# A per-token scale ratio, the first silus next to each other, and an earlier forget gate in a streaming-encoder block on one core

## The chip, the core and the metric

The kernel runs on one core of a Trainium2 chip. A core has TensorE (PE, matrix products, with PEld for its weight loads), VectorE (DVE), ScalarE (ACT), GpSimd (POOL) and SyncE (SP), each with its own queue that it takes in order, and 16 DMA engines that all queues share. SP issues the loads of weights, POOL some small or broadcast transfers. The metric is the device time of one execution in microseconds (us), as the median of several runs; the profile shows one execution of its own.

## What is computed

One layer of an encoder block on 256 tokens of 1024 features, in float32:

```python
x = x + 0.5 * rmsnorm(swiglu(rmsnorm(x, g1), ffn1_w_in, ffn1_w_down), g2)   # FFN 1, 2816 wide
q_a, f_a, i_a, g_a, q_b, k_b, v_b, f_b, gates = split(rmsnorm(x, g3) @ w_in)
A = rmsnorm(hgrn2(q_a, f_a, i_a)) * silu(g_a)        # gated linear recurrence, 8 heads
B = fox_attention(q_b, k_b, v_b, f_b + bias)         # causal; logits get the running sums of log f
y = sigmoid(gate_A) * (A @ w_branch_a) + sigmoid(gate_B) * (B @ w_branch_b)
x = x + rmsnorm(y @ w_out)
x = x + rmsnorm(cross_attention(rmsnorm(x), rmsnorm(mem)))
x = x + 0.5 * rmsnorm(swiglu(rmsnorm(x), ffn2_w_in, ffn2_w_down))           # FFN 2
# swiglu(h, w_in, w_down): gate, up = split(h @ w_in); (silu(gate) * up) @ w_down
# fox: c = cumsum(log_sigmoid(f_b + bias)); s[t, s'] = q.k / sqrt(128) + c[t] - c[s']
```

## The kernel before

**Weights.** Each float32 operand is split into a rounded part `hi` and a remainder `lo`, and a product is made of three: hi·hi, hi·lo and lo·hi. A unit of weights is 128x1024: `load_split` (L141) lets SP load it into one of 4 `raw` buffers (L148), ACT cast it to `hi` (L150) and DVE subtract to get `lo` (L152); there are 8 buffers for each of `hi` and `lo`. The subtraction gives `raw` back, which lets SP issue the next load. An entry in `hold` for a unit queues its cast and its subtraction behind two given instructions of ACT and DVE (`behind`); this orders the issue only, and only against instructions of the same engine.

**Order.** A scheduler orders each engine's queue by the program's order and by when it thinks inputs are ready. `tc.high_priority()` moves instructions ahead of others, `tc.issue_after(ins)` queues what follows on `ins`'s engine behind it, and `after(i)` does both against the i-th matmul in the log of PE.

**FFN.** `ffn` (L424) works in chunks of 256 of the 2816 hidden columns, 4 units each, 11 chunks. FFN 1 begins with `act_first`, which makes chunks 0 and 1 in all four `acc` banks while the first weights arrive, and then chunk 2 in the two `mm` banks. A chunk's sums are turned into activations by `act_evac` (L444): ACT's silu (L446) of the gate, scaled by the token's root-mean-square factor, then DVE's product with the other half (L449 or L451) into a tile `at`. `flush` (L432) has PE transpose `at` (L441) and ACT and DVE split the result into `act`, which `down` multiplies with the down weights `w_dn`. `h` counts the two halves of 128 tokens. `TOKS` lists the chunks made by tokens (`act_tok`), `PAIRS` those made two at a time by `act_pair`, a fast product of 2x2 blocks with seven block products in place of eight: FFN 1 has pairs from chunks 4, 6 and 9, FFN 2 from 3, 6 and 9.

A pair combines both halves of the tokens, which have different scales in each token. So `pair_inputs` (L520) first multiplies the second half of `xf` by the ratio of the halves' scales, `rho` (L528), and `act_evac` undoes a ratio `q` later. `row_of` (L354) makes the scales into a row: DVE transposes a 128x64 tile (L357), POOL writes it to memory (L359) and reads it back into all 128 partitions (L361). `rho` is then a reciprocal (L522) and a product (L523) on 128x128; `q` is the same ratio on 128x1 (L525, L526). In `act_pair` the third of four results is `c00` (L636), and its silu and `at` follow; behind a pair that is not followed by another pair comes a chunk by tokens.

**Recurrence and attention.** After FFN 1 the projections follow, with the recurrence's levels (1, 2, 4 to 128) between them: `Rec.grow` multiplies on DVE (L991), `Rec.keep` copies on ACT (L1030, L1034, L1037). The forget logits of the attention are made by `forget` (L1062: ACT's exponential and logarithm, L1070, L1071) and summed by `forget_sums` (L1073) in three DVE instructions (L1074, L1079 twice), whose result POOL writes to memory as `cd` (L1080). POOL later reads `cd` back as `ct` (L1167), `cbc` (L1169) and `cbm` (L1173); `cbc` and each of two `cbm` are 512 KB, broadcast to 128 partitions into buffers of the pool `m4`, which has 21 of 128x1024.

The recurrence's output is summed in `acc` banks, squared on ACT (L290), and multiplied into `G` by DVE (L1159); only then are the banks free for the scores of the attention's second half (L1199), which the rest of the attention reads. The second half of the `v_b` weights is cast meanwhile.

Of the kernel before, what the change touches and what calls it, by code (L numbers as in the profile page):

```python
# [11 lines left out]
F32 = mybir.dt.float32  # L12
# [3 lines left out]
ALU = mybir.AluOpType  # L16
AX = mybir.AxisListType

P = 128
# [4 lines left out]
FC = 256  # L24
GF = 344
NFF = D_FF // FC
# [49 lines left out]
_AT = {}  # L76
# [8 lines left out]
def block_kernel(ctx: ExitStack, tc: tile.TileContext, wts, head_in, gf_in, x_in, mem_in, memT_in, cols, rows, fbias, masks, out):  # L85
    nc = tc.nc
    V, S, G, PE = nc.vector, nc.scalar, nc.gpsimd, nc.tensor

    cp = ctx.enter_context(tc.tile_pool(name="consts", bufs=1))
    wp = ctx.enter_context(tc.tile_pool(name="weights", bufs=4))  # L90
    mp = ctx.enter_context(tc.tile_pool(name="data", bufs=21))
    sp = ctx.enter_context(tc.tile_pool(name="small", bufs=8))
# [16 lines left out]
    def nm(s):  # L109
        count[0] += 1  # L110
        return f"{s}_{count[0]}"
# [21 lines left out]
    evicted = []  # L133
    hold = {}
# [115 lines left out]
    def bc(a, shape, dim):  # L250
        return a.unsqueeze(dim).to_broadcast(shape)
# [89 lines left out]
        return r  # L341


    facs = cp.tile([P, 4, 64], F32, name="facs")
    G.memset(facs, 0.0)
    fac = [facs[:, i] for i in range(4)]

# [3 lines left out]
    def x_halves(h):  # L351
        return [xs[:, h, 0:512], xs[:, h, 512:]]

    def row_of(cols2):  # L354

        runs = sp.tile([P, 64], F32, tag="runs", name=nm("runs"), bufs=1)
        V.transpose(runs, cols2)  # L357
        rd = dp.tile([2, 4, 32], F32, name=nm("rd"))
        G.dma_start(rd.rearrange("h k t -> k h t"), runs[0:P:32].rearrange("k (h t) -> k h t", h=2))  # L359
        row = sp.tile([P, T], F32, tag="row", name=nm("row"), bufs=2)  # L360
        G.dma_start(row, rd.rearrange("h k t -> (h k t)").partition_broadcast(P))  # L361
        return row

    def gain_split(X, kb, src, g, a=0, b=T, first=False):
# [59 lines left out]
    def ffn(w_in, w_dn, X, r2, n_tok, i_row, first_half, second_half=None):  # L424

        acts = {}
        late = []
        ats = {}  # L430

# [12 lines left out]
        def act_evac(ps, c, h, r=None, q=None):  # L444
            sg = sp.tile([P, FC], F32, tag="c1", name=nm("sg"), bufs=7)
            silu = S.activation(sg, ps[:, :FC], AF.Silu, scale=r2[h] if r is None else r).ins  # L446
            a = sp.tile([P, FC], F32, tag="c1", name=nm("at"), bufs=7)
            if q is None:
                V.tensor_tensor(out=a, in0=ps[:, FC:], in1=sg, op=ALU.mult)  # L449
            else:  # L450
                V.scalar_tensor_tensor(out=a, in0=ps[:, FC:], scalar=q, in1=sg, op0=ALU.mult, op1=ALU.mult)  # L451
            ats[c, h] = a
            if h == 1:
                late.append(c)
            return silu
# [61 lines left out]
                V.tensor_tensor(out=t[:, 2 * i : 2 * i + 2], in0=x[:, :, 0], in1=x[:, :, 1], op=ALU.add)  # L517
            return t

        def pair_inputs():  # L520
            rho = sp.tile([P, P], F32, tag="c1", name=nm("rho"), bufs=7)
            V.reciprocal(rho, row[:, :P])  # L522
            V.tensor_tensor(out=rho, in0=row[:, P:], in1=rho, op=ALU.mult)  # L523
            q = s1(name="q")
            V.reciprocal(q, r2[1])  # L525
            V.tensor_tensor(out=q, in0=r2[0], in1=q, op=ALU.mult)  # L526
            for k in range(2):
                V.tensor_tensor(out=xf[k][:, :, P:], in0=xf[k][:, :, P:], in1=bc(rho, [P, 4, P], 1), op=ALU.mult)  # L528
            a, b, d, e = (xf[k][:, :, h * P : h * P + P] for h in range(2) for k in range(2))
            ss = [m4([P, 2, 4, P], n="ss") for _ in range(2)]  # L530
            de, aed, ad, baed = (t[:, i] for t in ss for i in range(2))
            V.tensor_tensor(out=de, in0=d, in1=e, op=ALU.subtract)
            V.tensor_tensor(out=aed, in0=de, in1=a, op=ALU.subtract)
            V.tensor_tensor(out=ad, in0=a, in1=d, op=ALU.subtract)
            V.tensor_tensor(out=baed, in0=b, in1=aed, op=ALU.add)
            out = {}
            for n, x in (("de", de), ("aed", aed), ("baed", baed), ("ad", ad), ("e", e)):
                t = m4([P, 2, 4, P], F32R, "sx")
                split(t[:, 0], t[:, 1], x)
                out[n] = t  # L540
            return out, q
# [16 lines left out]
        def act_pair(c, between):  # L558
            sx, q = pairs_in

            def of(n):
                return lambda kk: (sx[n][:, 0, kk], sx[n][:, 1, kk])

            def of_x(k):
                return lambda kk: (X.hi(4 * k + kk, 0, P), X.lo(4 * k + kk, 0, P))

            def splits(t):
                u = []
                for r in t:
                    p = parts_of()  # L570
                    split(p[0], p[1], r)
                    u.append(p)
                return u

            def raws(k, n):
                t = [wp.tile([P, D], F32, tag="raw", name=nm("raw"), bufs=4) for _ in range(2)]
                for j in range(2):
                    more(t[j], c, k, n, j, None)
                return t

            def add(t, o):
                for x, y in zip(t, o):
                    V.tensor_tensor(out=x, in0=x, in1=y, op=ALU.add)  # L583

            def product(ps, stat, u, start):
                for kk in range(4):
                    ah, al = stat(kk)
                    wh, wl = blk(u, kk)
                    for i, (x, y) in enumerate(((ah, wh), (ah, wl), (al, wh))):
                        MM(ps, x, y, start=start and kk == 0 and i == 0, stop=kk == 3 and i == 2, skip_group_check=not start)  # L590

            def step_between():
                if between:
# [12 lines left out]
            for _ in range(2 if c == 3 else 1):  # L606
                step_between()
            b4 = mm()
            product(b4, of("de"), splits(sums), True)
            S.copy(p5, b4)  # L610
            step_between()
            raw = raws(1, 1)
            add(sums, raw)
            product(b1, of("aed"), splits(sums), False)
            S.copy(v, b1)
            step_between()
            product(b4, of("baed"), splits(raw), False)
            add(both, raw)
            with tc.high_priority():
                t = half_tile("c01")  # L620
                V.tensor_tensor(out=t, in0=b4, in1=v, op=ALU.subtract)
                act_evac(t, c, 0)
            product(b1, of("ad"), splits(both), False)
            S.copy(w, b1)
            with tc.high_priority():
                t = half_tile("c11")
                V.tensor_tensor(out=t, in0=p5, in1=w, op=ALU.subtract)
                act_evac(t, c, 1, r2[0], q)
            step_between()
            b0 = trp()  # L630
            raw = raws(1, 0)
            product(b0, of_x(1), splits(raw), True)
            add(sums, raw)
            with tc.high_priority():
                t = half_tile("c00")
                V.tensor_tensor(out=t, in0=p1, in1=b0, op=ALU.add)  # L636
                act_evac(t, c + 1, 0)
            step_between()
            product(b1, of("e"), splits(sums), False)
            with tc.high_priority():  # L640
                silu = act_evac(b1, c + 1, 1, r2[0], q)
            if c + 1 == NFF - 1:
                table(silu)
            while between:
                step_between()
# [10 lines left out]
        for h in range(2):  # L656
            m = len(log)
            for c in range(n_tok):
                act_tok(c, h)
            if h == 0 and n_tok:  # L660
                second_half(m)
                row = row_of(fac[3])
                if pairs:
                    xf = [pair_joined(k) for k in range(2)]
        accs = None
        done = 0
        if callable(r2):
            outs = act_first((0, 1), acc)
            r2 = r2()
            chunk(w_in, 2)  # L670
            row = row_of(fac[2])
            for c in range(2):
                acts[c] = m4([P, 2, 2, T], F32R, "act")
                for h in range(2):
                    with tc.issue_after(casts[-1]):
                        act_evac(outs[c][h], c, h)
            n_tok = 2
        for c in range(n_tok, NFF):
            if c - 1 in pairs:
# [16 lines left out]
            elif c == 2 and first_half:  # L696
                n = len(log)
# [410 lines left out]
    for si, ms in enumerate(SETS):  # L1108
# [11 lines left out]
                for r in recs:  # L1120
                    r.keep(m, LEVELS.index(m) if m < 64 else None)
        if si == FG:
            with tc.issue_after(recs[1].grown):
                forget_sums()
        if si < 2:
            with tc.high_priority(), tc.issue_after(gf_last[R_GROW[si]]):
# [457 lines left out]
```

## Time and profile before

| | us |
|---|---|
| median of 3 runs | 778.22 |
| lowest and highest run | 776.54, 779.0 |
| the profiled execution, its own time | 779.33 |
| its span, first to last instruction | 777.2 |
| PE busy, weight loads busy | 764.9, 647.1 |
| DVE busy | 646.1 |
| ACT busy | 503.2 |
| POOL busy | 15.7 |
| mean granted TensorE clock | 0.998 |

PE's busy time holds the matmuls' own waits in its pipeline; whether it stands still is seen best from the distance between the starts of matmuls. In rows of instructions the columns are start and duration in us, engine, line, operation, output and inputs, shape and count; in brackets, the engine's idle time just before, and what ended it.

### The profile page before, as it was taken

How to read it: one execution, taken by the hardware profiler on the slowest of the kernel's cores; microseconds unless marked ns; L12 is line 12 of the kernel's file. 1: busy time of each engine (PE TensorE's matmuls, PEld its weight loads, DVE VectorE, ACT ScalarE, POOL GpSimd, SP SyncE). 2: the span in 40 equal slices, each digit the busy share in tenths (PEclk: the TensorE clock that was granted, in tenths of full speed). 3: DMA queues.
4: the chain of work that ended last, by engine and by line, in shares of the span. 5: the costliest groups of instructions: out<-in, count | busy, mean ns of one | idle time of the engine just before them, and what ended most of it. 6: DMA issues, size and time to landing. Idle time of an engine off the chain costs nothing.

```text
span 777.2 us, 11694 instructions
## 1 busy us (share of the span) xinstructions
PE 764.9 (98%) x4326; PEld 647.1 (83%) x4326; DVE 646.1 (83%) x975; ACT 503.2 (65%) x816; POOL 15.7 (2%) x39
## 2 busy tenths in 40 slices
PE   9999999999999999999999999999999999999996
PEld 8878888877888998888788888889888888888885
DVE  6699999988778898969777655886579899999973
ACT  7676666677775669547676444863668567675762
POOL 0000000000000100210000000000000000000000
PEclk9999999999999999999999999999999999999999
DMA  9764657366755535643767555456075725658231
GB/s 343 237 244 159 221 180 298 109 217 205 221 177 146 183 134 177 204 182 133 259 238 255 176 176 192 148 178 222 22 245 177 258 85 176 258 177 318 101 135 55
DMA packets 44505, 148.06 MB, mean 191 GB/s; under 512 B 5144, under 2 KB 8864, under 8 KB 44448
## 3 DMA queue, kind: packets, MB, share of 16 engines
q1 hardware_dynamic: 43168, 144.83, 53.7%
q0 software_dynamic: 848, 2.12, 1.1%
q8 instruction: 34, 0.56, 0.3%
q10 hardware_dynamic: 432, 0.37, 0.2%
q14 instruction: 23, 0.19, 0.1%
HBM read 146.24 MB, written 1.06 MB: 190 GB/s over the span
## 4 chain that ended last, share of the span: by engine, by line
PE 68%; DVE 21%; DMA 4%; issue 3%; ACT 3%; DVEq 0%; ACTq 0%; SPq 0%
PE mm L99 34%; PE acc L99 30%; DVE lo L152 5%; DVE lo L171 5%; DMA raw<-in_wts_dram 3%; DVE sraw L583 3%; PE tr L99 2%; ACT hi L150 1%; DVE qf L991 1%; PE tr L382 1%; DVE k L991 1%; PE tr L441 1%; DMA sraw<-in_wts_dram 1%; DVE act L171 1%; ACT f L1029 0%
## 5 line engine op out<-in xcount | busy, mean ns | idle before, releaser
L152 DVE TENSOR_TENSOR lo<-raw,hi 128x1024 fp32r<-128x1024 f32 (+1 forms) x204 | 241.0, 1200 | 35.7 <-ACT hi L150 30.6
L150 ACT CAST hi<-raw 128x1024 fp32r<-128x1024 f32 (+1 forms) x204 | 206.9, 1035 | 67.9 <-PE mm L99 30.6
L99 PE MATMUL mm<-hi,hlT 128*128 128x512 f32 (+1 forms) x688 | 209.4, 382 | 0.1
L99 PEld LDWEIGHTS mm<-hi,hlT 128*128 128x128 f32 x688 | 127.2, 188 | 22.8 <-issue 0.5
L99 PE MATMUL mm<-lo,hlT 128*128 128x512 f32 (+1 forms) x344 | 130.5, 382 | 0.0
L99 PE MATMUL acc<-hi,act 128*128 128x512 f32 x352 | 113.7, 391 | 0.0
L170 ACT CAST hi<-sraw 128x1024 fp32r<-128x1024 f32 x60 | 62.8, 1053 | 32.1 <-DVE sraw L583 23.2
L99 PE MATMUL mm<-hi,sx 128*128 128x512 f32 x240 | 77.7, 390 | 0.0
L99 PEld LDWEIGHTS acc<-hi,act 128*128 128x128 f32 x352 | 66.1, 188 | 13.4 <-ACT hi L150 0.2
L99 PEld LDWEIGHTS mm<-lo,hlT 128*128 128x128 f32 x344 | 64.6, 188 | 11.2 <-DVE lo L152 0.5
L171 DVE TENSOR_TENSOR lo<-sraw,hi 128x1024 fp32r<-128x1024 f32 x60 | 71.9, 1222 | 2.2 <-ACT hi L170 2.0
L99 PE MATMUL acc<-lo,act 128*128 128x512 f32 x176 | 70.0, 398 | 0.3 <-DVE lo L152 0.3
L99 PE MATMUL acc<-hlT,hi 128*128 128x512 f32 x256 | 64.4, 393 | 0.0
L99 PEld LDWEIGHTS mm<-hi,sx 128*128 128x128 f32 x240 | 45.0, 188 | 9.8 <-ACT sx L170 0.2
L99 PEld LDWEIGHTS acc<-hlT,hi 128*128 128x128 f32 x256 | 46.1, 189 | 8.3
L99 PE MATMUL mm<-lo,sx 128*128 128x512 f32 x120 | 46.8, 390 | 0.0
L583 DVE TENSOR_TENSOR sraw<-sraw,raw 128x1024 f32<-128x1024 f32 x36 | 43.0, 1222 | 0.0
L99 PEld LDWEIGHTS acc<-lo,act 128*128 128x128 f32 x176 | 33.1, 188 | 7.3 <-DVE lo L152 1.1
L99 PEld LDWEIGHTS acc<-hlT,lo 128*128 128x128 f32 x256 | 35.0, 190 | 2.5
L99 PE MATMUL acc<-hlT,lo 128*128 128x256 f32 x256 | 36.2, 283 | 0.0
L171 DVE TENSOR_TENSOR lo<-raw,hi 128x1024 fp32r<-128x1024 f32 x24 | 28.5, 1222 | 0.0
L170 ACT CAST hi<-raw 128x1024 fp32r<-128x1024 f32 x24 | 24.6, 1050 | 3.3 <-DMA raw<-in_wts_dram 3.0
(288 smaller groups left out, 1196.1 us busy)
## 6 DMA issues: line engine op xcount, KB each, us to landing
raw<-in_wts_dram SPq DMA_DIRECT2D x223, 512.0 KB, 4.4
sraw<-in_wts_dram SPq DMA_DIRECT2D x24, 512.0 KB, 6.5
raw<-in_gf_dram SPq DMA_DIRECT2D x12, 344.0 KB, 3.8
head<-in_head_dram SPq DMA_DIRECT2D x7, 392.0 KB, 7.3
grow<-in_rows_dram SPq DMA_DIRECT2D x4, 512.0 KB, 5.8
xs<-in_x_dram SPq DMA_DIRECT2D x2, 512.0 KB, 7.7
cbm<-cd POOLq DMA_DIRECT2D x2, 512.0 KB, 10.9
brow<-in_rows_dram SPq DMA_DIRECT2D x4, 256.0 KB, 3.6
```

Source lines behind the costliest of these rows:

```text
L99: log.append(PE.matmul(*args, **kw).ins)
L150: casts.append(S.copy(h, r).ins)
L152: V.tensor_tensor(out=l, in0=r, in1=h.bitcast(F32), op=ALU.subtract)
L170: a = S.copy(hi, src)
L171: b = V.tensor_tensor(out=lo, in0=src, in1=hi.bitcast(F32), op=ALU.subtract)
L382: PE.transpose(blocks[-1][1], src(kb), ident)
L441: PE.transpose(trv[:, j, h * P : (h + 1) * P], ats[c, h][:, j * P : (j + 1) * P], ident)
L583: V.tensor_tensor(out=x, in0=x, in1=y, op=ALU.add)
L991: self.grown = V.tensor_tensor(out=tv, in0=tv, in1=other, op=ALU.mult).ins
```

## The change

Four edits. `row_of` takes a number of halves; a new `ratio` makes the ratio on 128x1 columns, with one more reciprocal, writes it into a fifth slice of `facs`, and has `row_of` transpose and broadcast that alone (128x32 and half the bytes in the DMAs), so that `pair_inputs` multiplies by the row as it is; these multiplications are queued behind the last product `at` made so far. In FFN 1 the casts of the units 0 and 1 of `w_dn` and of chunk 3 are queued behind the last of the first four silus. In a pair that isn't followed by another one, the casts of units 1 to 3 of the chunk by tokens behind it, and their subtractions, are queued behind the silu and the `at` of `c00`. `forget_sums` gets high priority.

```diff
-    facs = cp.tile([P, 4, 64], F32, name="facs")
+    facs = cp.tile([P, 5, 64], F32, name="facs")
...
-    def row_of(cols2):
+    def row_of(cols2, n=2):
-        runs = sp.tile([P, 64], F32, tag="runs", name=nm("runs"), bufs=1)
+        runs = sp.tile([P, 64], F32, tag="runs", name=nm("runs"), bufs=1)[:, : 32 * n]
         V.transpose(runs, cols2)
-        rd = dp.tile([2, 4, 32], F32, name=nm("rd"))
+        rd = dp.tile([n, 4, 32], F32, name=nm("rd"))
...
-        G.dma_start(row, rd.rearrange("h k t -> (h k t)").partition_broadcast(P))
+        G.dma_start(row[:, : n * P], rd.rearrange("h k t -> (h k t)").partition_broadcast(P))
...
+            evs.append((silu, v.ins))
...
-        def pair_inputs():
-            rho = sp.tile([P, P], F32, tag="c1", name=nm("rho"), bufs=7)
-            V.reciprocal(rho, row[:, :P])
-            V.tensor_tensor(out=rho, in0=row[:, P:], in1=rho, op=ALU.mult)
+        def ratio():
+            cols1 = facs[:, 4, 32 * bool(i_row) : 32 * bool(i_row) + 32]
             q = s1(name="q")
             V.reciprocal(q, r2[1])
             V.tensor_tensor(out=q, in0=r2[0], in1=q, op=ALU.mult)
+            V.reciprocal(cols1[:, 0:1], q)
+            return q, row_of(cols1, 1)
+
+        def pair_inputs():
             for k in range(2):
-                V.tensor_tensor(out=xf[k][:, :, P:], in0=xf[k][:, :, P:], in1=bc(rho, [P, 4, P], 1), op=ALU.mult)
+              with tc.issue_after(evs[-1][1]):
+                V.tensor_tensor(out=xf[k][:, :, P:], in0=xf[k][:, :, P:], in1=bc(row[:, :P], [P, 4, P], 1), op=ALU.mult)
...
                 act_evac(t, c + 1, 0)
+            if c + 2 not in pairs and c + 2 < NFF:
+                for i in range(1, 4):
+                    hold[_AT[w_in] + 4 * (c + 2) + i] = evs[-1]
...
-                row = row_of(fac[3])
+                q, row = ratio()
...
-            row = row_of(fac[2])
+            q, row = ratio()
             for c in range(2):
                 acts[c] = m4([P, 2, 2, T], F32R, "act")
                 for h in range(2):
                     with tc.issue_after(casts[-1]):
-                        act_evac(outs[c][h], c, h)
+                        silu = act_evac(outs[c][h], c, h)
+            for i in range(2):
+                hold[_AT[w_dn] + i] = hold[_AT[w_in] + 12 + i] = (silu, evicted[-1][1])
...
         if si == FG:
-            with tc.issue_after(recs[1].grown):
+            with tc.high_priority(), tc.issue_after(recs[1].grown):
                 forget_sums()
```

More of the change, by code (lines that the diff above doesn't have):

```diff
@@ L352, in x_halves @@
         return [xs[:, h, 0:512], xs[:, h, 512:]]
-    def row_of(cols2):
-        runs = sp.tile([P, 64], F32, tag="runs", name=nm("runs"), bufs=1)
+    def row_of(cols2, n=2):
+        runs = sp.tile([P, 64], F32, tag="runs", name=nm("runs"), bufs=1)[:, : 32 * n]
         V.transpose(runs, cols2)
-        rd = dp.tile([2, 4, 32], F32, name=nm("rd"))
-        G.dma_start(rd.rearrange("h k t -> k h t"), runs[0:P:32].rearrange("k (h t) -> k h t", h=2))
+        rd = dp.tile([n, 4, 32], F32, name=nm("rd"))
+        G.dma_start(rd.rearrange("h k t -> k h t"), runs[0:P:32].rearrange("k (h t) -> k h t", h=n))
         row = sp.tile([P, T], F32, tag="row", name=nm("row"), bufs=2)
-        G.dma_start(row, rd.rearrange("h k t -> (h k t)").partition_broadcast(P))
+        G.dma_start(row[:, : n * P], rd.rearrange("h k t -> (h k t)").partition_broadcast(P))
         return row
@@ L428, in ffn @@
         acts = {}
+        evs = []
         late = []
@@ L448, in act_evac @@
             if q is None:
-                V.tensor_tensor(out=a, in0=ps[:, FC:], in1=sg, op=ALU.mult)
+                v = V.tensor_tensor(out=a, in0=ps[:, FC:], in1=sg, op=ALU.mult)
             else:
-                V.scalar_tensor_tensor(out=a, in0=ps[:, FC:], scalar=q, in1=sg, op0=ALU.mult, op1=ALU.mult)
+                v = V.scalar_tensor_tensor(out=a, in0=ps[:, FC:], scalar=q, in1=sg, op0=ALU.mult, op1=ALU.mult)
+            evs.append((silu, v.ins))
             ats[c, h] = a
```

## Prediction

> **What bounds the kernel now.** I read the page's first lines, then busy time by stretches, then TensorE's (PE's) own timeline wherever a stretch was not full.
>
> ```profile
> span 777.2 us, 11694 instructions
> ...
> PE 764.9 (98%) x4326; PEld 647.1 (83%) x4326; DVE 646.1 (83%) x975; ACT 503.2 (65%) x816; POOL 15.7 (2%) x39
> ```
>
> ```profile
> 60.00:160.00 100.00, 100.00 (x454) 82.58 (x454) 99.45 (x102) 67.13 (x84) 0.00 (x0) 1.00 0.56 196
> ...
> 340.00:344.00 4.00, 2.11 (x15) 1.80 (x15) 3.57 (x15) 2.79 (x6) 0.00 (x0) 1.00 0.02 6
> ...
> 600.00:760.00 160.00, 160.00 (x732) 131.95 (x731) 149.12 (x181) 105.07 (x140) 1.16 (x2) 1.00 0.53 187
> ```
>
> The columns after the stretch are its length and the busy us of PE, PEld, DVE, ACT and POOL, then clock, DMA share and GB/s. PE is full in most of FFN 1 (454 matmuls in 100 us, 0.22 each) and in all of FFN 2 shown here, at a granted clock of 1.00. So work taken from DVE, ACT or a queue pays only where PE itself stands still. The change touches three such places. Two lie at the start of FFN 1, one at the forgetting attention.
>
> The first place: four transposes of the activations (L441), behind the third chunk's product.
>
> ```profile
> 37.76 1.07 PE L99 MATMUL mm<-hi,hlT 128*128 128x512 f32 x4
> 39.13 0.41 PE L441 MATMUL tr<-ident,at 128*128 128x128 f32 x2 [0.30 <-DVE at L449]
> 40.50 0.44 PE L441 MATMUL tr<-ident,at 128*128 128x128 f32 x2 [0.97 <-DVE at L449]
> ```
>
> Four matmuls at 0.23 from 37.76 end their turn at 38.67; the transposes begin at 39.13, so 0.46 is lost. Two transposes take 0.24 of PE's turn, and the next two begin at 40.50 and not at 39.37: 1.13. Together **1.59 us**, on the products `at` of L449, which need the silus of L446.
>
> ```profile
> 27.09 0.46 ACT L446 ACTIVATE sg<-acc,facs 128x256 f32<-128x256 f32 x1
> 30.19 1.05 ACT L150 CAST hi<-raw 128x1024 fp32r<-128x1024 f32 x1 [2.64 <-DMA raw<-in_wts_dram]
> ...
> 35.74 1.05 ACT L150 CAST hi<-raw 128x1024 fp32r<-128x1024 f32 x1 [4.12 <-DMA raw<-in_wts_dram]
> ...
> 38.48 0.48 ACT L446 ACTIVATE sg<-acc,facs 128x256 f32<-128x256 f32 x1
> ```
>
> ACT takes its queue in order. Casts that wait 2.64 and 4.12 us for weights to land stand between the silus, and the fourth silu runs at 38.48, over 11 us behind the first, though the sums it reads are of the same product.
>
> The second place is PE's change from chunk 3 to the first pair.
>
> ```profile
> 57.84 0.99 PE L99 MATMUL mm<-hi,hlT 128*128 128x512 f32 x2
> ```
>
> ```profile
> 57.79 0.43 DVE L449 TENSOR_TENSOR at<-mm,sg 128x256 f32<-128x256 f32 x1
> ```
>
> ```profile
> 130.03 0.62 PE L99 MATMUL mm<-hi,hlT 128*128 128x512 f32 x2
> ```
>
> Two matmuls elsewhere take 0.62, here 0.99: **0.37** late, on the `mm` bank that DVE's `at` frees at 58.2.
>
> The third place is the second half's scores (L1199).
>
> ```profile
> 340.51 0.38 PE L99 MATMUL tr<-k_b,q_b 128*128 128x128 f32 x2
> 342.78 0.39 PE L99 MATMUL acc<-kp,qp 128*128 128x256 f32 x1 [1.89 <-DVE G L1159]
> ```
>
> ```profile
> 327.68 9.88 DMA raw<-in_wts_dram
> ...
> 338.54 0.69 ACT junk L290 x2
> ```
>
> The scores could begin at 340.73 and begin at 342.78, **2.05 us** late. They need an `acc` bank that L1159 frees; L1159 needs the squares of L290; these stand in ACT's queue behind a cast whose weights were under way for 9.88 us, until 337.56.
>
> **The change, part by part.**
>
> *Silus together.* The holds on units 0 and 1 of chunk 3 and of the down weights keep exactly the casts above behind the fourth silu. The silus then run from 27.09, 0.46 to 0.48 each; the last may wait a little for the first product's end, and all are done by about 29.5. The casts lose nothing, since the first lands at 30.17. The hold's second part queues a DVE subtraction behind a gain split long done. The products `at` move into time in which DVE had nothing:
>
> ```profile
> 36.82 1.23 DVE L152 TENSOR_TENSOR lo<-raw,hi 128x1024 fp32r<-128x1024 f32 x1 [3.99 <-ACT hi L150]
> ...
> 38.57 0.41 DVE L449 TENSOR_TENSOR at<-acc,sg 128x256 f32<-128x256 f32 x1
> 38.90 1.22 DVE L152 TENSOR_TENSOR lo<-raw,hi 128x1024 fp32r<-128x1024 f32 x1
> ```
>
> So PE gains the 1.59. What is late next is the down product, which needs the subtraction of 36.82, done at 38.05; with PE at its second half of the transposes around 39.1, that is in time. If the DMA were later by over a microsecond the cover would be gone and the gain with it.
>
> *Ratio per token.* Away go, in each FFN, two instructions on 128x128:
>
> ```profile
> L522 DVE RECIPROCAL rho<-row x2: 943/946/948, 45.0 to 629.2; 128x128 f32<-128x128 f32 x2
> L523 DVE TENSOR_TENSOR rho<-row,rho x2: 280/282/284, 47.0 to 631.2; 128x128 f32<-128x128 f32 x2
> ```
>
> In comes one 128x1 reciprocal ahead of the transposition and the two DMAs of `row_of`, which become half as large. I take it for less than the 0.28 of the 128x128 product; in FFN 1 it runs at 25 us, and DVE's idle 3.99 us before 36.82 hides it, as the row is used only from 45 on. Only FFN 1 can use the saving: PE is full in FFN 2 (row 600 to 760), so I cost it at nothing there. In FFN 1, DVE comes to 57.79 sooner by two `at` of 0.33 (start to start, 38.57 to 38.90) and by 0.95 and 0.28 less the same overlap of 0.08 each: 0.66 + 1.07 = 1.73. PE comes 1.59 sooner, so 0.14 of the 0.37 is won too. Bounds: 0.37 won if DVE stays ahead throughout, 1.59 lost (PE's whole gain, given back at the bank) if DVE comes no sooner; I take 0.14, which the rows give. The order of the multiplication of `xf` behind the last `at` agrees with the order that DVE has now.
>
> The Trainium skill's page "VectorE: DVE Perf Modes", in its section on the TRN2 errata, prices an SBUF instruction at 58 cycles plus its elements at 0.96 GHz, by which 128x128 is an estimated 0.19 us, reciprocal or not. The rows say 0.946 and 0.282, so the measurement decides; by the page's figure the two would save 0.39, DVE would come 1.05 sooner and the start would gain 1.05 in place of 1.73.
>
> *Sums of the forget gate.* At high priority the three DVE instructions may run as soon as their inputs and L991 of level 32 are done.
>
> ```profile
> 300.23 0.67 DVE L991 TENSOR_TENSOR qf<-qf,aux 128x512 f32<-128x512 f32 x1
> 302.89 0.42 DVE L224 TENSOR_TENSOR q_b<-mm,plo 128x256 f32<-128x256 f32 x1 [1.98 <-ACT plo L222]
> ...
> 317.55 0.40 DVE L1074 SCALAR_TENSOR_TENSOR fa<-fz,fa 8x256 f32<-8x256 f32 x1
> ```
>
> ```profile
> 299.06 0.42 ACT L1071 ACTIVATE fa<-fa 8x256 f32<-8x256 f32 x1
> ```
>
> Their input is there at 299.48, and DVE idles for 1.98 us from 300.90: three instructions of 0.40 to 0.47 fit. So they move by some 16 us at no cost, and with them everything POOL has queued behind them:
>
> ```profile
> 319.42 0.53 POOL L1080 DMA_DIRECT2D cd<-cc  x1 [47.79 <-DVE cc L1079]
> ```
>
> ```profile
> raw<-in_wts_dram SPq DMA_DIRECT2D x4, 512.0 KB, 7.9
> cbm<-cd POOLq DMA_DIRECT2D x2, 512.0 KB, 10.9
> cbc<-cd POOLq DMA_DIRECT2D x1, 512.0 KB, 8.1
> ```
>
> ```profile
> raw<-in_wts_dram SPq DMA_DIRECT2D x7, 512.0 KB, 3.2
> ```
>
> The first three are the issues from 323 to 329 (last column: median us to landing), the fourth those from 300 to 318, before POOL's broadcasts. Weights that go beside the 1.5 MB of broadcasts take 7.9 us, others 3.2. Sixteen microseconds sooner the broadcasts are over by about 320, and the cast that now waits until 337.56 can run some 3 us sooner (three others stand before it); squares, root and L1159 follow by at least the 2.05 that PE lacks. I take 2.05. Bounds: 2.05 if it all goes, 0 if `cbc` and `cbm` wait for buffers (they share the 21 `m4` buffers; by the code 16 are taken at 303 to 312, so the three they need are free), and below that what the broadcasts do to the loads they now meet (a rival, below).
>
> *Later casts in the pairs.* Units 1 to 3 of the token chunk behind a pair now follow the silu of the pair's third product. In FFN 1:
>
> ```profile
> 124.69 0.51 ACT L446 ACTIVATE sg<-c,facs 128x256 f32<-128x256 f32 x1
> ```
>
> ```profile
> 127.10 2.35 DVE L152 TENSOR_TENSOR lo<-raw,hi 128x1024 fp32r<-128x1024 f32 x2
> ```
>
> The silu comes 0.5 sooner and two casts of 1.05 come behind it; the last subtraction still ends near 129.5. PE comes to the fourth unit with the second of the two matmuls at 130.03 (quoted above), so the cover is some 0.8 us. I cost it at nothing; if the cover goes, PE waits for each unit's subtraction (the slower rival).
>
> **Sum.** 1.59 + 0.14 + 2.05 = 3.8 us. The profiled execution took 779.33 (span 777.2 and 2.1 around it), so 775.5; the median of the runs is 778.22, 1.1 below it, so **774.4**.
>
> **Rivals.**
>
> *The collision moves (25%).* The broadcasts now meet the loads of 307 and 308, the last two units of `q_b`. For it speaks that the cast at 310.51 waits for its weights already:
>
> ```profile
> 310.51 1.05 ACT L150 CAST hi<-raw 128x1024 fp32r<-128x1024 f32 x1 [0.88 <-DMA raw<-in_wts_dram]
> ...
> 314.83 0.39 ACT L222 COPY plo<-mm 128x256 f32<-128x256 f32 x1
> ```
>
> ```profile
> 320.98 1.32 PE L99 MATMUL mm<-hlT,hi 128*128 128x512 f32 x5
> ```
>
> With 7.9 for 3.2 (4.7 late; 6.7 at the worst, 9.88) the copy of 314.83 ends at 319.9 to 321.9, DVE's add takes 0.42, and PE wants that bank at 320.98: none to 1.3 us is lost, and weights further on can be late too. With 1.3 lost and half of the 2.05 not won the time is 776.7; the same if the buffers hold the broadcasts back (1.73 won: 776.5). Against it: most loads of 312 to 318 have until 320.
>
> The Trainium skill's "DMA: Bandwidth & Descriptors", section "Issuing engines are not separate DMA queues", says that transfers of all issuing engines end on the same 16 DMA engines and interleave; by that rule the collision moves and does not vanish. The rows 7.9 against 3.2 agree.
>
> *Given back (15%).* The engines' orders come out anew around the moved instructions, and PE's next waits grow by what was won: 778.2.
>
> *The held casts starve PE, slower (12%).* The holds in the pairs, at three places (chunk 8 of FFN 1, chunks 5 and 8 of FFN 2). An idle ACT must leave ready casts standing until the silu; if two other casts of 1.05 and the 0.5 silu then come first, the units are 2.6 late, 1.8 more than the cover, and as their raw buffers go back 2.6 later, the loads behind can add up to that. With half of it the price is 3.1 a place, 9.3 in all: 783.7. It decides from 6.1 us in all, 2.0 a place. Against it: DVE, which makes the second half of each unit, is busy until 129.45 as it is, so that casts 0.5 to 1 us later cost it little.
>
> **Chances and range.** The forecast has 48%, within 773.0 to 775.8. A difference of 0.3% (2.3 us) is about what the measurement can tell from none, the three runs being 776.54 to 779.0. Faster by more than that: the forecast and a part of the moved collision, 0.56. The same: the rest of it and the gain given back, 0.31. Slower: 0.13. The range goes from 772.8 to 779.2, which takes in all but the slower case and a tail.
>
> **What would show it.** Four silus of L446 in a row from 27 and no wait of L441 on `at`; no L522, L523; L1074 near 301, `cbm` landed by 321, loads of 324 to 328 back at 3 to 4 us, L290 near 336, and no wait on G. Against me: casts at 310 to 318 that wait on DMA with PE idle at 321; PE idle on `lo` of L152 in chunk 8; or L1169 waiting for a buffer.

## The result, and the profile after

The changed kernel takes 776.23 us (median of 13 runs, 774.9 to 777.99) against 777.97 for the kernel before (13 runs, 776.04 to 779.0): a ratio of 0.9981, 95% interval [0.9971, 0.9991]. It is faster by about 1.5 us, where 3.8 were forecast.

The two profiled executions show more than that: before's took 779.33, the one after 774.9, so they lie 4.4 apart. Before's is slower than any of its 13 runs, and the one after is the fastest of its kernel's. So no gain is read from these two traces alone.

The page's first lines after:

```profile
span 772.8 us, 11694 instructions
...
PE 762.8 (99%) x4326; PEld 646.8 (84%) x4326; DVE 645.4 (84%) x973; ACT 505.1 (65%) x816; POOL 16.9 (2%) x39
```

DVE has two instructions fewer. Lines of the code from 441 on stand 1 to 11 lines further down (L441 is L442, L991 is L1002, L1074 is L1085). ACT's, DVE's and PE's rows of the start:

```profile
26.46 1.56 ACT L447 ACTIVATE sg<-acc,facs 128x256 f32<-128x256 f32 x4
29.68 1.06 ACT L150 CAST hi<-raw 128x1024 fp32r<-128x1024 f32 x1 [1.66 <-DMA raw<-in_wts_dram]
```

```profile
29.46 1.41 DVE L450 TENSOR_TENSOR at<-acc,sg 128x256 f32<-128x256 f32 x4
```

```profile
38.10 0.60 PE L442 MATMUL tr<-ident,at 128*128 128x128 f32 x4
...
55.60 0.62 PE L99 MATMUL mm<-hi,hlT 128*128 128x512 f32 x2
```

The silus run in a row, the four transposes start as one row, and the two matmuls that took 0.99 near 57.84 take the usual 0.62. So at the first two places PE no longer stands still. PE's waits, with the total, the times and the longest:

```profile
PE mm L99 <- DVE lo L152: 2.0, 1, 2.0
PE tr L99 <- PEq L1584: 0.8, 1, 0.8
PE acc L99 <- DVE lo L152: 0.6, 2, 0.3
```

The wait on `G` is gone as well, but the first row is new. On PE and on DVE it looks like this:

```profile
306.68 0.87 PE L99 MATMUL mm<-hlT,lo 128*128 128x256 f32 x6
309.52 0.39 PE L99 MATMUL mm<-hlT,lo 128*128 128x256 f32 x1 [1.97 <-DVE lo L152]
```

```profile
297.73 0.41 DVE L1085 SCALAR_TENSOR_TENSOR fa<-fz,fa 8x256 f32<-8x256 f32 x1
...
300.13 0.40 DVE L1090 TENSOR_TENSOR_SCAN cc<-ones,fa 8x128 f32<-8x128 f32 x1
...
302.30 1.22 DVE L152 TENSOR_TENSOR lo<-raw,hi 128x1024 fp32r<-128x1024 f32 x1
...
303.77 1.22 DVE L152 TENSOR_TENSOR lo<-raw,hi 128x1024 fp32r<-128x1024 f32 x1
304.90 0.69 DVE L1002 TENSOR_TENSOR k<-k,tq 128x512 f32<-128x512 f32 x1
...
308.25 1.22 DVE L152 TENSOR_TENSOR lo<-raw,hi 128x1024 fp32r<-128x1024 f32 x1
```

The seventh matmul was due some 0.12 behind the sixth, at 307.40, and needs the subtraction of the fourth unit of the second half's `k_b`, which ends at 309.47. Its input was there long before: casts and subtractions come in the same order, 208 of each, and the cast of this unit is the second of this row of ACT, done at 301.66:

```profile
299.66 2.00 ACT L150 CAST hi<-raw 128x1024 fp32r<-128x1024 f32 x2
```

So it waited for its place in DVE's queue and not for its weights. In the kernel before, the same subtraction is the second of a pair directly ahead of the multiplications of level 64:

```profile
306.06 2.35 DVE L152 TENSOR_TENSOR lo<-raw,hi 128x1024 fp32r<-128x1024 f32 x2
308.33 0.69 DVE L991 TENSOR_TENSOR k<-k,tq 128x512 f32<-128x512 f32 x1
```

In the queue drawn up with the sums in it, that subtraction stands behind the four multiplications, a subtraction for `kp` and an addition for `q_b`. Five starts 0.60 apart and one of 0.34 are 3.3 us.

### The profile page after: what moved, and what is told of

Its sections match the earlier page's. It is cut to its first block, busy times and chain, and to the rows that moved or that the text cites. A ratio compares the mean times of both kernels' runs of the same rounds, so it can differ in the third digit from the quotient of the medians.

```text
span 772.8 us, 11694 instructions
## 1 busy us (share of the span) xinstructions
PE 762.8 (99%) x4326; PEld 646.8 (84%) x4326; DVE 645.4 (84%) x973; ACT 505.1 (65%) x816; POOL 16.9 (2%) x39
## 4 chain that ended last, share of the span: by engine, by line
PE 88%; DVE 8%; ACT 2%; issue 1%; DMA 1%; DVEq 0%; ACTq 0%; SPq 0%
PE mm L99 44%; PE acc L99 37%; PE tr L99 5%; DVE lo L152 2%; DVE lo L171 1%; DVE sraw L589 1%; PE tr L442 1%; DVE qf L1002 1%; PE tr L382 1%; DVE k L1002 1%; DMA raw<-in_wts_dram 1%; ACT hi L150 1%; ACT f L1040 0%; PE tr L1232 0%; DVE aux L1031 0%
## 5 line engine op out<-in xcount | busy, mean ns | idle before, releaser
L152 DVE TENSOR_TENSOR lo<-raw,hi 128x1024 fp32r<-128x1024 f32 (+1 forms) x204 | 241.4, 1201 | 36.5 <-ACT hi L150 30.6
L99 PEld LDWEIGHTS mm<-lo,sx 128*128 128x128 f32 x120 | 22.5, 188 | 4.7
```

The lines of the kernel that those rows point to most:

```text
L99: log.append(PE.matmul(*args, **kw).ins)
L152: V.tensor_tensor(out=l, in0=r, in1=h.bitcast(F32), op=ALU.subtract)
```

## The experiments

Theory A: the gain forecast is real in all its parts, and the early sums give back about 2 us by this order of DVE's queue. Rival B: the sums' gain was never there (the waits on `G` differ from execution to execution, and the broadcasts only hinder other loads), and the silus and the ratio make the whole result. The table sets all versions together. Each ratio is to the kernel before on the same chip: e1 to e4 and e13 to e15 ran on one chip, e5 to e8 on a second, e9 to e12 on a third. The letters are the edits in the kernel: S the silus together, R the ratio per token, P the casts held in the pairs, F the sums at high priority. "Lead" is how much sooner a matmul starts than the matmul of the same number in PE's order does in the trace of before. From it is taken the same difference at the 25th matmul (near 6.9), since up to there the traces start from 0.8 us sooner to 0.3 us later than before's. The columns name the time of the matmul in before. A lead comes from one execution, a ratio from 5 to 13.

| kernel | edits | ratio to before, 95% interval | lead at 59 | 198 | 304 | 312 | 383 |
|---|---|---|---|---|---|---|---|
| changed | SRPF | 0.9981 [0.9971, 0.9991] | 2.1 | 2.4 | 2.4 | 0.4 | 3.9 |
| e12, again | SRPF | 0.9979 [0.9966, 0.9992] | 2.1 | 2.2 | 2.2 | -1.2 | 2.0 |
| e1 | SRP | 0.9976 [0.9963, 0.999] | 1.9 | 2.2 | 2.1 | 2.2 | 1.8 |
| e2 | SRP, F later | 0.9998 [0.9986, 1.001] | 2.1 | 1.5 | 1.4 | 1.5 | -0.6 |
| e3 | F | 0.9995 [0.9983, 1.0006] | 0.2 | 0.2 | 0.2 | -2.9 | -0.1 |
| e4 | S | 1.001 [0.9996, 1.0024] | 1.7 | 0.9 | 0.6 | 0.7 | 1.2 |
| e5 | R | 1.0014 [1.0003, 1.0025] | -0.2 | 0.1 | 0.2 | 0.2 | 1.9 |
| e8 | P | 1.0002 [0.999, 1.0015] | 0.9 | 0.9 | 0.8 | 0.9 | 1.4 |
| e6 | SR | 0.9992 [0.9981, 1.0003] | 1.9 | 0.9 | 0.9 | 0.9 | -1.5 |
| e7 | SRP, F between | 0.9956 [0.9943, 0.9969] | 2.1 | 1.9 | 2.0 | 1.3 | 4.8 |
| e9 | SR, F between | 0.9958 [0.9943, 0.9972] | 2.1 | 2.0 | 1.9 | 1.4 | 4.3 |
| e10 | RP, F between | 0.9989 [0.9979, 0.9999] | 0.6 | 0.4 | 0.5 | -0.1 | 3.2 |
| e11 | SP, F between | 0.9965 [0.9952, 0.9979] | 1.9 | 0.3 | 0.3 | -0.4 | 3.1 |
| e15 | F between | 0.9966 [0.9953, 0.9979] | -0.3 | -0.4 | -0.3 | -1.0 | 2.4 |
| e13 | SRPF, level 64 held | 0.997 [0.9956, 0.9985] | 2.1 | 1.3 | 1.2 | 0.5 | 1.6 |
| e14 | SRPF, second ahead | 0.9979 [0.9966, 0.9991] | 2.1 | 1.9 | 1.9 | -0.1 | 1.8 |

### The sums taken out, put later, and alone

e1 takes the priority back:

```diff
-            with tc.high_priority(), tc.issue_after(recs[1].grown):
+            with tc.issue_after(recs[1].grown):
                 forget_sums()
```

> The changed kernel without the high priority of the forget gate's sums. Theory A (given back): the sums, put early into DVE's queue, push the subtraction for the fourth unit of the second k_b chunk behind the multiplications of level 64, and PE waits 2.0 us for it; this pays back what the scores win. Then here that wait is gone, the scores wait about 2 us on L1159 again (and the transposes of G about 1 us), the start of FFN 1 keeps its 1.7, and the time is 776.0 to 776.6 against 778.0 before. Rival B (the broadcasts slow the loads): the same here, but PE's wait near 307 would show a cast waiting on a DMA that took over 5 us. Rival C (the holds in the pairs cost what is missing): PE waits on lo in chunk 8 or 5, and the time is 777 or more.

Without the early sums the kernel takes 777.25 (before on that chip 778.48): a ratio of 0.9976, as theory A had it, and no slower than with them. PE's waits in e1:

```profile
PE tr L382 <- DVE lT L370: 2.4, 1, 2.4
PE acc L99 <- DVE G L1170: 0.9, 1, 0.9
```

There is no wait on `lo` near 308, while the scores' wait on `G` is back, with 0.9. The first row is one that the prediction had left out: the transposes of `G` near 378, which wait for a gain split. So the early sums win something behind 320 and lose at least as much at 308.

e2 moves them one level later, behind the multiplications of level 64:

```diff
-FG = 3
+FG = 4
```

> The changed kernel with the sums behind level 64 and not level 32 (FG = 4): some 9 us later than in the changed kernel, still some 6 sooner than before, with all subtractions for k_b ahead of them in DVE's queue. Theory A: no wait of PE on lo near 307, none on L1159, 2 us faster than the changed kernel: 774.0 to 774.8. Rival B: the broadcasts now meet the loads of v_b, these take over 7 us, and PE waits near 320 or at the scores: 776 or more.

Theory A's expectation failed: 778.54. No wait stands at 308, but the broadcasts now go beside the loads of 317 to 323, and two casts wait for them:

```profile
323.67 1.05 ACT L150 CAST hi<-raw 128x1024 fp32r<-128x1024 f32 x1 [2.26 <-DMA raw<-in_wts_dram]
...
326.87 1.06 ACT L150 CAST hi<-raw 128x1024 fp32r<-128x1024 f32 x1 [1.88 <-DMA raw<-in_wts_dram]
```

```profile
PE tr L382 <- DVE lT L370: 2.5, 1, 2.5
PE acc L99 <- DVE G L1170: 2.4, 1, 2.4
```

These rows fit the collision that the prediction named as a rival, at a place where it has a price: against e1 the kernel loses 1.7 us by the ratios. Putting the broadcasts sooner by 7 us (`cd` is issued at 312.19 in place of 319.42) is no gain.

e3 has the priority alone; the rest of the change is undone (`forget_sums` as in the change, all other lines as before).

> The kernel before with the early sums alone. Theory A: the wait at the scores (2.05) and at the transposes of G (1.1) goes, a wait of 2.0 on the subtraction comes: 1 us faster than before, 776.5 to 777.5. Had the sums been free, as predicted, 2 us faster: 775.9. Rival B: as A, but with loads of over 5 us ahead of the casts that PE waits for.

778.33 against 778.48, a ratio of 0.9995, so not even the 1 us of theory A: the waits on `G` and at the transposes of `G` are gone, the lead falls by 3.1 between 304 and 312, and this row is there again:

```profile
PE mm L99 <- DVE lo L152: 2.0, 1, 2.0
```

### The other parts alone, and in company

e4, e5 and e8 keep one part each and undo the rest; e6 keeps the silus and the ratio:

```diff
 e4: +                hold[_AT[w_dn] + i] = hold[_AT[w_in] + 12 + i] = (silu, evicted[-1][1])
 e5: +                q, row = ratio()
 e8: +                    hold[_AT[w_in] + 4 * (c + 2) + i] = evs[-1]
 e6: the lines of e4 and e5
```

> The kernel before with the four silus together alone (holds on units 0 and 1 of the down weights and of chunk 3). As predicted: the wait of 1.59 at the transposes goes, the wait at the bank near 57 grows, as DVE has won only 0.66 and not 1.73: about 1.0 us faster, 776.7 to 777.3. If the start is worth all of 1.6: 776.4.

> The ratio per token alone, with the silus, the later casts and the sums as before. Theory A (the start's gains are separate, and the ratio's worth is what DVE saves ahead of PE's wait on the mm bank near 57): the four transposes near 39 still wait on the products at (0.46 and 1.13), the bank's wait near 57 goes, since DVE comes 1.1 sooner and PE no sooner; that is 0.37, so 0.9995 of the time before, within 0.9985 to 1.0005. Theory B (DVE is late by less than a microsecond at many places of FFN 1 from 60 on, so 1.1 us less of its work there also takes away the small waits at 80 to 190 that gave the silus' gain back when they came alone): 1.5 to 2 us, 0.9975 to 0.998, and the transposes near 180 start at once.

> The silus together and the ratio per token, without the sums and without the casts held in the pairs. Theory A (the held casts do nothing): the same as with the held casts and without the sums, 0.9976, so 0.9965 to 0.9985, with 2.2 us or more won by 60 and not given back by 300. Theory B (the held casts bring part of that): 0.9985 to 1.0, with waits at 80 to 190 that the kernel with the held casts lacks.

> The casts held in the pairs alone. Theory A (they do nothing): 0.9995 to 1.0005, the waits of before at 39, 57, 183, 342 and 378 all there. Theory B (the silu of the pair's third product no longer waits behind casts, so later transposes start sooner): 0.998 to 0.999. Theory C, the slower rival of the prediction (the held casts leave PE without weights): PE waits on subtractions near 130 and 175 and in FFN 2, 1.002 or more.

None of the three parts alone is faster, against the expectation of 1 us for e4. The ratio alone is even slower, by 1.1 us [0.2, 1.9], which neither theory of e5 had; its trace, of the fastest of its executions (777.46), does not show where. The silus alone win their lead at the start (1.7 at 59), but it shrinks to 0.9 by 198; the ratio alone has no lead, since the transposes still wait on `at`. The single lead of 0.9 in e8 came at the transposes too (0.6 waited there in place of 1.3), and its time is that of before. e6, at 0.9992, did not come to the 0.9976 of its theory A. Its trace, of its slowest execution (780.69), lost 1.0 of its lead between 59 and 198, which would have spoken for the held casts; but its interval and e1's overlap, and later it waited 2.1 on `G` and 1.9 at the next transposes. These waits differ too much between executions (0.4 to 2.4 on `G`, 0.8 to 2.5 at the transposes, in before and the six kernels without sums at the early place) for a part worth 1 us to be read beside them. A better base was needed.

### The sums between the subtractions

e7 queues the sums behind the second of the four subtractions and level 64 behind the fourth; a list `los` keeps the subtractions of L152:

```diff
-            V.tensor_tensor(out=l, in0=r, in1=h.bitcast(F32), op=ALU.subtract)
+            los.append(V.tensor_tensor(out=l, in0=r, in1=h.bitcast(F32), op=ALU.subtract).ins)
...
+            if c == 1 and name == "k_b":
+                kb_lo = los[-4:]
...
-            with tc.issue_after(gf_last[1, 1]) if si == 1 else nullcontext():
+            with tc.issue_after(gf_last[1, 1]) if si == 1 else tc.issue_after(kb_lo[3]) if ms[-1] == 64 else nullcontext():
...
-            with tc.high_priority(), tc.issue_after(recs[1].grown):
+            with tc.high_priority(), tc.issue_after(kb_lo[1]):
                 forget_sums()
```

> The whole change, but the sums are queued behind the second subtraction of the second half's k_b weights (instead of ahead of it), and the multiplications of level 64 behind the fourth. Theory A (the early sums cost 2 us only because they push those subtractions back, which holds buffers of the loads): the wait of 1.97 near 308 shrinks below 0.5, the scores and the transposes of G still find their inputs ready, and the kernel gains 1.5 to 2 on the whole change: 0.9955 to 0.9965 of the time before. Theory B (wherever the 1.5 MB of broadcasts go, the loads beside them are late by as much, and the wait only moves): a wait of 1.5 to 2.5 us near 308, 320 or 340, and 0.9975 to 0.9985.

Theory A holds. The median is 774.73 (5 runs, 773.99 to 775.32), before on that chip 778.21: this version beats both kernels. The seven matmuls on `lo` go in one row, and 0.61 is left, on level 64:

```profile
307.01 0.99 PE L99 MATMUL mm<-hlT,lo 128*128 128x256 f32 x7
307.85 1.06 PE L99 MATMUL acc<-qf,k 128*128 128x128 f32 x8
309.52 1.16 PE L99 MATMUL acc<-qf,k 128*128 128x128 f32 x8 [0.61 <-DVE qf L1003]
```

The subtractions and level 64 stand on DVE in the order of before (L153 is L152 and L1003 is L1002 here):

```profile
304.11 2.34 DVE L153 TENSOR_TENSOR lo<-raw,hi 128x1024 fp32r<-128x1024 f32 x2
306.38 0.67 DVE L1003 TENSOR_TENSOR k<-k,tq 128x512 f32<-128x512 f32 x1
```

No wait on `G` is left. The broadcasts still hinder the loads, as after the change, where loads and broadcasts of 311 to 317 took:

```profile
raw<-in_wts_dram SPq DMA_DIRECT2D x4, 512.0 KB, 7.2
cbm<-cd POOLq DMA_DIRECT2D x2, 512.0 KB, 7.1
```

In e7 the same loads took 6.0, and PE did not wait for them. So B's "the wait only moves" is refuted here.

On this base, parts were taken away again, and the changed kernel was timed beside them (e9 without the held casts, e10 without the silus' hold, e11 with `rho` back, e12 the changed kernel):

```diff
 e9:  -                    hold[_AT[w_in] + 4 * (c + 2) + i] = evs[-1]
 e10: -                hold[_AT[w_dn] + i] = hold[_AT[w_in] + 12 + i] = (silu, evicted[-1][1])
 e11: -                q, row = ratio()
```

> The kernel with the sums between the subtractions, less the casts held in the pairs. Theory A (the held casts are worth nothing, as forecast): as with them, 0.995 to 0.9963 of the time before. Theory B (with the silus and the ratio in place, DVE and ACT are what FFN 1 waits for at 85 to 185, and without the holds the casts stand ahead of the silus there; one trace without the sums lost 1.2 more there): about 1.2 lost, 0.9965 to 0.998, with PE's waits between 85 and 185 to match.

> The kernel with the sums between the subtractions, less the holds that bring the first four silus together. Theory A (the transposes' 1.6 is a loss of its own and adds to the others): about 1.6 lost, 0.997 to 0.9985 of the time before, and the lead over before at 190 shrinks from about 1.9 to 0.3. Theory B (FFN 1 from 60 to 160 goes at DVE's pace, 99.45 busy in 100, so that PE's start counts only as far as DVE starts sooner, 0.66): 0.5 to 0.8 lost, 0.996 to 0.9968, lead at 190 about 1.2.

> The kernel with the sums between the subtractions, less the ratio per token (the reciprocal and the product on 128x128 are back). Theory A (the forecast's working: DVE comes 1.07 later to the bank near 57 and PE waits there): 0.9 to 1.2 lost, 0.9967 to 0.9975, as one wait near 57. Theory B (no wait there in the trace with the silus alone, but small waits from 85 on give the lead back, which needs DVE's saving): 1.0 to 1.5 lost, 0.9968 to 0.998, as waits of 0.2 to 0.5 between 85 and 185.

> The changed kernel once more, beside the three above on one chip. Both theories: 0.997 to 0.999 of the time before, and a wait of 1.5 to 2.5 on the subtraction near 308; the kernels with the sums between the subtractions should be below it by what they keep of 2. If its median were at 0.996 instead, the gain seen with the sums between the subtractions would be the chip's and not the order's.

The held casts are worth nothing (0.9958 against 0.9956). Without the silus' hold 2.6 us are lost by the ratios (0.0033 of 778) and 1.5 by the lead at 198; the forecast's 1.59 lies within what the intervals allow (theory A of e10 by the lead, with a little more lost than it had). Without the ratio per token 0.7 is lost by the ratios, less than either theory of e11 had and within the intervals, and 1.6 of the lead at 198, although the lead at 59 is the same (1.9 against 2.1). So its saving is not collected at the bank near 57 in these traces but, if at all, beyond it. The stretch from 60 to 160, in the changed kernel and in e11:

```profile
60.00:160.00 100.00, 100.00 (x454) 82.19 (x453) 99.59 (x104) 69.04 (x86) 0.00 (x0) 1.00 0.55 192
```

```profile
60.00:160.00 100.00, 99.64 (x448) 81.22 (x447) 98.87 (x103) 67.40 (x84) 0.00 (x0) 1.00 0.57 196
```

In the same 100 us PE makes 454 matmuls in the one and 448 in the other; six at 0.22 are 1.3 us. The nine traces with both the silus and the ratio have 450 to 454 (e7 450), the two with the silus and without the ratio 448 and 449 (e11, e4); so part of the 1.3 is a difference between executions. DVE (fourth pair of columns) is busy for 99 of the 100 in both. That a lead of PE's is given back in pieces where DVE does not come sooner too would fit this; it is argued, not shown.

e12 gives the changed kernel's result again (776.61, 0.9979). On the same chip e9 takes 774.87, so the 1.7 us between them (0.0023 or 1.8 us between e12 and e7) are not the chip's.

Two kernels tell which part of the order costs: e13 has only the line with `kb_lo[3]` (level 64 behind the fourth subtraction), e14 only the line with `kb_lo[1]` (the second subtraction ahead of the sums). e15 has e7's edit on the kernel before.

> The changed kernel with only the multiplications of level 64 queued behind the fourth subtraction; the sums stay ahead of the second. Theory A (the late load is the cost: the fourth cast waits for weights that SP could only issue after the late second subtraction, and ran to 307.87 in the trace): the subtraction ends near 309.1 in place of 309.47, the wait near 308 is still 1.2 to 2.2, and the time is 0.997 to 0.9985 of before. Theory B (the four multiplications and what stands with them between are the cost): the wait is below 0.5 and the time 0.9952 to 0.9965.

> The changed kernel with only the sums queued behind the second subtraction; the fourth stays behind level 64. Theory A (late load): the load comes 1.3 sooner, the fourth cast no longer waits, but its subtraction still stands behind four multiplications of 0.69; were the load all, the wait would be below 0.7 and the time 0.9955 to 0.9968. Theory B (the order against level 64): the wait stays at 1.5 to 2.5 and the time at 0.9975 to 0.9985.

> The kernel before with the sums between the subtractions and nothing else of the change. Theory A (the forecast's 2.05 at the scores, and the transposes of G that it left out): 2 to 3.2 us won in the stretch from 300 to 385, less about 0.6 near 308, so 0.9968 to 0.9982 of the time before. Theory B (PE's gain there is the other edits', and the sums alone give nothing, as with the sums queued sooner): 0.999 to 1.0005.

The first rows below are PE's in e13, the second in e14 (L153 is L152 there):

```profile
307.85 1.00 PE L99 MATMUL mm<-hlT,lo 128*128 128x256 f32 x7
308.69 1.06 PE L99 MATMUL acc<-qf,k 128*128 128x128 f32 x8
310.38 1.16 PE L99 MATMUL acc<-qf,k 128*128 128x128 f32 x8 [0.64 <-DVE qf L1003]
```

```profile
307.81 0.87 PE L99 MATMUL mm<-hlT,lo 128*128 128x256 f32 x6
310.67 0.39 PE L99 MATMUL mm<-hlT,lo 128*128 128x256 f32 x1 [1.99 <-DVE lo L153]
```

By the traces theory B of these two holds and A falls: the wait on `lo` goes with level 64 alone and stays with the second subtraction alone. (A rested on taking the cast that ended at 307.87 for that of the fourth unit; in e13 the cast that waits on its load runs at 308.36, when this subtraction is done, so that cast belongs to a later unit.) The time of e13 does not decide: 0.997 lies in A's range and not in B's, between the changed kernel and e7, and the intervals reach both. Its trace waits 1.9 at the transposes of `G`, e7's not at all. Whether that difference is the order's or the execution's is open.

The leads of the table say the same of all versions with early sums. Between 304 and 312 the lead falls by 2.0 to 3.4 where level 64 stands ahead of the fourth subtraction (changed, e12, e3, e14), and by 0.5 to 0.7 where it is held behind it (e7, e9, e10, e11, e13, e15).

e15 shows the forecast's third term by itself: 0.9966, or 2.6 us [1.6, 3.7] won by the sums in the mended order, slightly more than theory A had; in the trace the lead grows by 3.5 between 312 and 383. Beside e3, on the same chip, it shows the price of the order in time: the same early sums, 0.9995 in the one order and 0.9966 in the other, 2.3 us apart, and the intervals don't overlap.

It also gives the other edits a second base. With the sums between, and the held casts taken as nothing, the silus alone add nothing (e11, 0.9965), the ratio alone costs 1.8 us (e10, 0.9989), and both together win 0.6 to 0.8 (e9, e7), which is within the intervals. Without early sums it is 0.8 lost (e4), 1.1 lost (e5) and 0.6 won (e6), or 1.9 with the held casts (e1). So on both bases silus and ratio together are 2.3 to 2.5 us better than their single effects add up to. What the ratio costs when it comes without the silus is open; the trace of e10, too, is of its fastest execution.

## Why the prediction was half right

- **The first two places: right at the places, less certain in the time.** The transposes and the bank start on time, worth 2.1 at 59 where 1.73 was forecast: the bank gave all its 0.37 and not 0.14. By the ratios the edits there, with the held casts, bring 1.9 us [0.8, 2.9] without early sums (e1), but only 0.8 beside e15 (e7). The FFN 1 behind has to keep the lead, which the prediction did not ask, though it quoted the row with DVE at 99.45 in 100; at 198 the nine traces with both edits have 0.9 to 2.4 of it. Its bound of "1.59 lost (PE's whole gain, given back at the bank) if DVE comes no sooner" had the wrong place: without the ratio's saving the lead is kept past the bank, and half of it (e4) to most of it (e11) goes between 60 and 198. That the cause is DVE is argued, not shown. That the ratio alone makes the kernel slower (e5) the prediction did not see.
- **The sums at no cost: the step that failed.** "So they move by some 16 us at no cost" was wrong by about 2 us (1.8 between e12 and e7 and 2.3 between e3 and e15 by the ratios; 2.0 of PE's wait in the trace). The idle 1.98 us at 300.90 was there, and the sums are short (0.40 to 0.47). What was not priced is that the queue is drawn up anew, and that an instruction close to its need, the fourth subtraction, ended up behind 3.3 us of others. It had under 2 us to spare: in before it ended at 308.41, and the last of seven matmuls 0.12 apart, the one that needs it, started near 310.36 (PE's row below). This is the rival "given back" (15%), which the prediction left without a place.

```profile
309.64 0.99 PE L99 MATMUL mm<-hlT,lo 128*128 128x256 f32 x7
```

- **The scores' 2.05: right in size, wrong in its certainty.** In before's trace the wait was 1.9, in the traces of six other versions without the early place 0.4 to 2.4; the transposes of `G` behind it, 0.8 to 2.5, were left out. For both together, less the 0.6 that is left on level 64, e15 gives 2.6.
- **The collision: moved, and free here.** Loads of 311 to 317 took 7.2, near the 7.9 that the prediction's rival took, and loads of 322 to 327 again 3.4; no PE wait on them followed. In e2, with the broadcasts some 10 us later, PE's waits were longer. That transfers of all issuing engines interleave (the Trainium skill, "DMA: Bandwidth & Descriptors", section "Issuing engines are not separate DMA queues") agrees with the 7.1 of the broadcasts beside the 7.2 of the loads.
- **Enough free buffers: by this row wrong.** POOL waited 4.87 us for a matmul before it issued a broadcast; no wait of PE followed from it:

```profile
311.34 0.56 POOL L1184 DMA_DIRECT2D cbm<-cd  x1 [4.87 <-PE acc L99]
```

- **The held casts at nothing: right** (e7 and e9), and the slower rival built on them did not come.
- **FFN 2 at nothing: right for the changed kernel.** PE is as full as before, and its lead is 3.9 at 383 and at the end. (DVE's 145.93 us in place of 149.12 are mostly a matter of what falls into the stretch, 4 us sooner: over the whole span DVE has 0.7 us less.) In two kernels without the ratio, e4 and e11, the lead falls by 0.7 between 620 and 640, in e15, also without it, it doesn't; that is open.

```profile
600.00:760.00 160.00, 160.00 (x727) 132.00 (x727) 145.93 (x173) 103.65 (x137) 1.15 (x2) 1.00 0.51 178
```

- **The quoted price of 0.19 us: too low.** The rows have 0.282 and 0.946 for the two instructions. The section of the Trainium skill that the prediction quotes ("VectorE: DVE Perf Modes", the TRN2 errata) says itself, right behind the table row, that the row under-predicts.
- **The sum.** 1.59 + 0.14 + 2.05 is 3.8; with the order mended it is 3.4 [2.4, 4.4] (e7), and with 1.8 given back to the order 1.6 are left, and 1.5 were measured. That 3.4 comes so near 3.8 is in part luck: it holds the transposes of `G`, which the forecast left out, less the 0.6 on level 64, and by e15 the first two places give only 0.8 of it. The total in the mended order was forecast well, and one price, the order's, was missed.

## What to carry to other kernels

An instruction moved up in a queue has two prices: its own time, and what the scheduler swaps around it; so find, behind the new place, the instructions with less than a few microseconds to spare and pin them. Where an engine is busy for 99 of 100 us behind a stall, ask whether the lead won at the stall can be kept; here a part of it was lost again, for a reason that is argued only. Parts that win nothing or cost alone can win together, so undo one part from the best version, and add one to the kernel before as well.

## What was not expected of the hardware

The executions' spread went with the place of the sums: before ran from 776.43 to 781.73 beside e7 (29 runs), the changed kernel within 3.9 us (e12, 12 runs), but the kernels with the sums between the subtractions within 1.3 (e7, 5 runs), 1.5 (e9, 7 runs; e11, 10), 1.8 (e15, 6) and 2.2 (e10, 12). Waits on weights that share the DMA engines with broadcasts may be the larger part of the spread; it was not tested.

DVE instructions on one column took 0.14 to 0.22 us whatever they did. The product and the added reciprocal of that size:

```profile
L527 DVE TENSOR_TENSOR q<-facs,q x2: 153/156/159, 24.4 to 604.3; 128x1 f32<-128x1 f32 x2
L528 DVE RECIPROCAL facs<-q x2: 164/164/164, 24.6 to 604.5; 128x1 f32<-128x1 f32 x2
```

A reciprocal costs hardly more than a product on one column but 3.4 times as much on 128 (946 against 282 ns), so the ratio on columns takes DVE less time.
